# Two blocks with 32 experts on one core: fixed order of TensorE's side work, another place for the lasting slot, and loaded norm weights

## The chip, the cores and the metric

One core of a Trainium2 chip. The metric is the time of one execution on the device in microseconds (us). Engines are named as in the profile: PE is TensorE (matmuls; PEld its weight loads), DVE is VectorE, ACT is ScalarE, POOL is GpSimd, SP the engine whose queue issues the weight loads (SPq).

## The reference

256 tokens of width 1024 go through two transformer blocks in float32. The first is a hybrid layer (four mixers and a gated feed-forward part), the second has a pool and differential attention, cross attention and a mixture of experts, and a last RMS norm. The change touches only the mixture of experts and that norm:

```python
def clamped_swiglu(gu):
    gate, up = gu[..., :D_EXPERT], gu[..., D_EXPERT:]
    gate = jnp.minimum(gate, 7.0)
    up = jnp.clip(up, -7.0, 7.0)
    return (up + 1.0) * gate * jax.nn.sigmoid(1.702 * gate)

# 32 experts, each token goes to its top 4, gates = softmax over these four
hb = clamped_swiglu(xb @ w_gu[e] + b_gu[e])      # w_gu[e]: 1024 x 2048
yb = hb @ w_down[e] + b_down[e]                  # w_down[e]: 1024 x 1024
y = y.at[tok].add(yb * gate)
...
return rms_norm(x + y, final_norm_g)
```

All 32 experts' weights are read: 8 MB of gate/up and 4 MB of down weights each.

## The kernel before

The first three quarters of the text compute everything up to the router; the change leaves that alone but for one vector of norm weights (`load_vecs("v5", ...)`, line 577). The rest, from line 1320 on, is the expert stage.

**Tiles and products.** Each expert has 64 places for tokens (`CAP`). A gather (matmuls of the token rows `x_t` with a normalised one-hot matrix, lines 1459 and 1472) makes `xg`, the tokens of two experts at a time (`GR = 2`). The gate/up product "gu" (line 1524) runs over eight steps k; each step has four matmuls of 512 columns, and each shows as two instructions (eight per step, 64 per expert). ACT copies the result to `gs` (line 1532). `swiglu` turns it: `make(0)` and `make(1)` each transpose four blocks on PE (line 1541, tile "gte") and run seven operations on DVE and ACT (lines 1547 to 1555) into `u`. The down product "dn" (line 1567) has eight steps of two matmuls (32 instructions). `hilo` splits its result into `yh` (ACT, line 213) and `yl` (DVE, line 214), and `scatter` (line 1577) adds both to the four accumulators `acc` by a map `sT` that `turn_slots` makes on PE (lines 1444 to 1448, tile "ste").

**Order of an expert.** For expert e the text says: `make(0)`; the gate/up product of e + 1 with `make(1)` placed ahead of its step 1, the scatter of e - 1 ahead of step 3 and the slot map of e ahead of step 4; then the down product of e with, for even e, the two gathers for the next pair ahead of its steps 0 and 4. These places are the order of the text only. A planner in the framework chooses the real order of each engine by its own times and may move an instruction ahead of others. An *issue edge* (`with behind(m)`, which enters `tc.issue_after`) ties it: instructions of the block are put behind the given instruction on that instruction's engine; it adds no wait.

**Accumulators.** PSUM has eight banks here: four for `acc`, two of tag "mm", one "tr", one "y". gu uses both "mm"; dn uses "y"; transposes, slot maps and gathers use "tr", `make(1)` "y".

**Slots and loads.** Weights lie in a ring of 12 slots of 16 KB per partition (2 MB; `SLOTS`, `slot_tile`, line 1482), taken in turn. A gate/up set takes four, a down set two. SP's queue issues the loads (line 1494; the last piece of the last expert in three parts, line 1510), each when the readers of the slot's former content are done. Expert 30's `gs` must outlive the test below, and so is put into a slot of its own, "keep", taken just ahead of gu30; expert 30 and 31's remaining loads come behind it.

**The end.** After expert 29 stands `overflow()`: if any expert has more than 64 tokens, a loop works the rest off (line 1617 holds the test; here no body is run, but each engine branches past it). Behind it come 16 matmuls that spread the last norm's weights over the partitions (line 1679, tile "gb"), expert 30's `make`, gu31, dn30, dn31, the last scatters and the norm (lines 1696 to 1708).

Of the kernel before, what the change touches and what calls it, by code (L numbers as in the profile page):

```python
# [22 lines left out]
P = 128  # L23
T = 256
D = 1024
# [4 lines left out]
CAP = 64  # L30
# [13 lines left out]
def kernel(ctx: ExitStack, tc: tile.TileContext, A, out, probe=None, stop=None):  # L44
    nc = tc.nc
    V, S, G, PE = nc.vector, nc.scalar, nc.gpsimd, nc.tensor
    ld = nc.sync.dma_start
    ldc = nc.sync.dma_start
# [8 lines left out]
    last = {}  # L57
# [5 lines left out]
    @contextmanager  # L63
    def behind(m):

        with ExitStack() as es:
            for ins in m.values():
                es.enter_context(tc.issue_after(ins.ins))
            yield
# [21 lines left out]
    def ps(name, tag="mm"):  # L91
        return pst["pool"].tile([P, 512], F32, tag=tag, name=name, bufs=pst["tags"][tag])
# [38 lines left out]
    vec = {}  # L131
# [138 lines left out]
    def half(h):  # L270
        return slice(h * 512, (h + 1) * 512)
# [169 lines left out]
    for g0, g1 in ((0, 388), (388, 774), (774, 1160)):  # L441
        n = g1 - g0
# [58 lines left out]
    def attention(name, qk, kchunk, vcol, bias, sink=None, extra=None, cq=None):  # L501
# [3 lines left out]
        for p in range(4):  # L505
# [36 lines left out]
            for j in range(2):  # L542
                ptr = ps(f"{name}t{p}{j}", "tr")
                for b in (1, 0):
# [3 lines left out]
                    for s in range(b + 1):  # L548
# [28 lines left out]
    v5 = load_vecs("v5", [("attn", r128(A["attn_norm_g_2"]), 8), ("xattn", r128(A["xattn_norm_g_2"]), 8),  # L577
                     ("memn", r128(A["mem_norm_g_2"]), 8), *(("ffn", A["ffn_norm_g_2"].rearrange("o (k p j) -> (o k) p j", p=P, j=2)[:, :, j], 4) for j in range(2)),
                     ("pscale", r128(A["pool_scale_2"]), 4), ("subln", A["subln_g_2"], 1),
                     ("fgattn", A["final_g"].rearrange("(c p) -> c p", p=P), 8),  # L580
                     ("last", A["final_norm_g_2"].rearrange("(c p) -> c p", p=P), 8)])


    qc = qk_group("foxqk", 1792, 8, 4)
# [836 lines left out]
    def one_hot(pos_cols, n, name):  # L1421

        s_ = small.tile([P, 2, n, 2, CAP], BF16, tag="S_", name=f"S{name}", bufs=1)
        io = iota_s.unsqueeze(1).unsqueeze(1).to_broadcast([P, n, 2, CAP])
        for b in range(2):
            pos = pos_cols[:, b, :].unsqueeze(2).unsqueeze(3).to_broadcast([P, n, 2, CAP])
            V.tensor_tensor(s_[:, b], io, pos, op=ALU.is_equal)
        return s_
# [10 lines left out]
    def turn_slots(s_, g3, name):  # L1439

        pt = ps(f"st{name}", "tr")
        for b in range(2):
            sd = s_[:, b].rearrange("p q s -> p (q s)")
            PE.matmul(pt[:, b * P:(b + 1) * P], sd, ident_b, start=True, stop=True)  # L1444
            PE.matmul(pt[:, T + 3 * b:T + 3 * b + 3], sd, g3[:, b], start=True, stop=True)  # L1445
        S.copy(sT, pt[:, :T])
        gs_ = small.tile([P, 1], F32, tag="gslot", name=f"gslot{name}")
        V.tensor_reduce(out=gs_, in_=pt[:, T:T + 6], axis=AX.X, op=ALU.add)
        return gs_
# [32 lines left out]
    def slot_tile():  # L1482

        rawc[0] += 1
        pool = slots[SLOTS[slot[0] % len(SLOTS)]]
        slot[0] += 1
        return pool.tile([P, 4 * D], F32, tag="raw", name=f"raw{rawc[0]}")
# [13 lines left out]
    def load_gu(src, ahead=()):  # L1501
        w = [t.rearrange("p (j c) -> p j c", j=2) for t in ahead]
        return (w + [piece(src, m, slot_tile(), 2) for m in range(len(w), 4)]).__getitem__

    def load_dn(src, parts=False):
        w = [piece(src, m, slot_tile(), 4) for m in range(2 - parts)]
        if parts:
            t = slot_tile().rearrange("p (j c) -> p j c", j=4)
            for a, b in ((0, 2), (2, 3), (3, 4)):
                ld(t[:, a:b, :], src[4 * P:8 * P, :].rearrange("(p j) c -> p j c", j=4)[:, a:b, :])  # L1510
            w.append(t)
        return w.__getitem__

    def gu_product(wt, xg, col, name, between=None):

        pgu = [ps(f"gu{name}_{n}") for n in range(2)]
        for k in range(8):
            for f in (between or {}).get(k, ()):
                f()
            if k % 2 == 0:  # L1520
                w = wt(k // 2)
            for n in range(2):
                for cg in range(2):
                    PE.matmul(pgu[n][cg * CAP:(cg + 1) * CAP, :], xg[:, k, col:col + CAP],  # L1524
                              w[:, k % 2, cg * D + n * 512:cg * D + (n + 1) * 512], start=k == 0, stop=k == 7)
        return pgu

    def gu_out(pgu, name, gs=None):
        if gs is None:
            gs = small.tile([P, D], F32, tag="gs", name=f"gs{name}", bufs=1)  # L1530
        for n in range(2):
            S.copy(gs[:, n * 512:(n + 1) * 512], pgu[n])  # L1532
        return gs

    def swiglu(gs, bcol, name, u_=u_):

        def make(h, tag="tr"):
            pt = ps(f"gt{name}_{h}", tag)
            for c in range(4):

                PE.transpose(pt[:, c * P:(c + 1) * P], gs[:, every(4, 4 * h + c)], ident)  # L1541
            pv = pt.rearrange("p (c q s) -> p c q s", c=4, q=2)

            g_, t_ = (gs[:, 512 * h + 256 * i:512 * h + 256 * (i + 1)].rearrange("p (c s) -> p c s", c=4)
                      for i in range(2))
            u = u_[:, h]
            V.tensor_tensor(g_, pv[:, :, 0, :],  # L1547
                            bcol[:, 4 * h:4 * h + 4].unsqueeze(2).to_broadcast([P, 4, CAP]), op=ALU.add)
            V.tensor_tensor(u, pv[:, :, 1, :],
                            bcol[:, 8 + 4 * h:12 + 4 * h].unsqueeze(2).to_broadcast([P, 4, CAP]), op=ALU.add)  # L1550
            V.tensor_scalar(g_, g_, 7.0, None, op0=ALU.min)  # L1551
            V.tensor_scalar(u, u, 7.0, -7.0, op0=ALU.min, op1=ALU.max)
            S.activation(t_, g_, AF.Tanh, scale=0.851)  # L1553
            V.scalar_tensor_tensor(u, u, 1.0, g_, op0=ALU.add, op1=ALU.mult)
            V.scalar_tensor_tensor(u, t_, 1.0, u, op0=ALU.add, op1=ALU.mult)
        return make

    def dn_product(wt, gslot, name, u_=u_, tag="y", between=None):

        po = ps(f"dn{name}", tag)  # L1560
        for k in range(8):
            for f in (between or {}).get(k, ()):
                f()
            if k % 4 == 0:
                w = wt(k // 4)
            for cg in range(2):
                PE.matmul(po[cg * CAP:(cg + 1) * CAP, :], u_[:, k // 4, k % 4, :],  # L1567
                          w[:, k % 4, cg * 512:(cg + 1) * 512], start=k == 0, stop=k == 7)
        hilo(yh, yl, po, scale=gslot() if callable(gslot) else gslot)

# [19 lines left out]
        st["xg"], *how = gather(norm_hot(pos_cols, GR, f"g{g}"), GR, f"g{g}")  # L1590
        return how

    def front(e, between):
        if e == EOVER + 1:

            st["keep"] = slot_tile()
        w = load_gu(w_gu[e], () if e else gu0)
        pgu = gu_product(w, st["xg"], (e % GR) * CAP, f"e{e}", between)

        return gu_out(pgu, f"e{e}", st["keep"][:, :D] if e == EOVER + 1 else None)  # L1600

    def slots_of(e):
        st["gslot", e] = turn_slots(one_hot(pos1[:, :, e:e + 1], 1, f"e{e}")[:, :, 0], gate3[:, :, e, :], f"e{e}")

    chunk, _ = group(0)
    first = {k: [lambda k=k: chunk(k + 1, k % 2 == 0, ("tr", "y")[(k + 1) % 2])] for k in range(1, 7)}
# [38 lines left out]

    for e in range(NE - 2):
        make = swiglu(gs, bgu[:, :, e], f"e{e}")
        make(0)
        between = {1: [lambda: make(1, "y")], 4: [lambda: slots_of(e)]}
        if e and e - 1 != EOVER:  # L1650
            between[3] = [scatter]
        gs = front(e + 1, between)
        wd = load_dn(w_dn2[e])
        if e == 15:
            load_b_down()
        if e == EOVER:

            wg1 = load_gu(w_gu[e1])
            wd0, wd1 = load_dn(w_dn2[e0]), load_dn(w_dn2[e1], parts=True)
        if e == 2:  # L1660
            counts()
        between = {}
        if e % GR == 0:
            _, four = group(e // GR + 1)
            between = {0: [lambda: four(0)], 4: [lambda: four(1)]}
        if e == 15:
            between = {4: [gates_down], 6: [add_b_down]}
        dn_product(wd, st["gslot", e], f"e{e}", between=between)

    scatter()  # L1670
    overflow()


    work = slot_tile()
    gb2 = work[:, D:2 * D]
    for h in range(2):
        pt = ps(f"gb2_{h}")
        for c in range(4):
            PE.matmul(pt[:, c * P:(c + 1) * P], vec["last"][:, 4 * h + c:4 * h + c + 1].to_broadcast([P, P]), ident,  # L1679
                      start=True, stop=True)  # L1680
        S.copy(gb2[:, half(h)], pt)
    make = swiglu(gs, bgu[:, :, e0], f"e{e0}")
    make(0)
    slots_of(e0)
    gs = gu_out(gu_product(wg1, st["xg"], (e1 % GR) * CAP, f"e{e1}", {1: [lambda: make(1)]}), f"e{e1}")
    u1 = slot_tile()[:, :2 * 4 * CAP].rearrange("p (h c s) -> p h c s", h=2, c=4)
    make1 = swiglu(gs, bgu[:, :, e1], f"e{e1}", u1)
    dn_product(wd0, st["gslot", e0], f"e{e0}", between={2: [lambda: make1(0)], 4: [lambda: make1(1)]})
    dn_product(wd1, lambda: st["gslot", e1], f"e{e1}", u_=u1, tag="mm",
               between={2: [scatter], 4: [lambda: slots_of(e1)]})  # L1690
    ssl = mp.tile([P, 3, 2], F32, name="ssl")
# [49 lines left out]
```

## Time and profile before

| | us |
|---|---|
| median of 3 runs (lowest, highest) | 1718.88 (1717.53, 1719.52) |
| profiled execution | 1718.83 |
| its span, first to last instruction | 1717.1 |
| PE busy | 1613.4 (94%) |
| DVE busy | 721.5 (42%) |
| ACT busy | 510.9 (30%) |
| POOL busy | 221.1 (13%) |
| HBM read | 524.95 MB |

The span is that of the profiled execution; the time measured for the same execution is 1.7 us longer. Busy time of PE counts pipelined matmuls with modelled ends. In the rows below "idle before" and "<-" name what ended an engine's wait. The expert stage runs from about 760 us to the end.

### The profile page before, as it was taken

To read this page: it belongs to the slowest core of one execution; us is meant where nothing else is said; L and a number is where in the kernel's file an instruction comes from. 1 tells how busy PE (TensorE), PEld (TensorE's weight loads), DVE (VectorE), ACT (ScalarE), POOL (GpSimd) and SP (SyncE) were. 2 spreads that over 40 slices of the span, in tenths; PEclk is the share of its full clock that TensorE was granted. 3 is DMA by queue.
4 is the path that set the end of the run, shared out by engine and by line. 5 is a ranking of instruction groups with operands and counts; after the bars stand their busy time and mean duration, and the time that the engine had idled before them with its cause. 6 is when DMAs were issued, how large, how long until landed. Compare 5 with 4: busy or idle time off the path is not lost. (4 is left out here: it accounts for less than half of the span.)

```text
span 1717.1 us, 23092 instructions
## 1 busy us (share of the span) xinstructions
PE 1613.4 (94%) x9269; PEld 1013.2 (59%) x9270; DVE 721.5 (42%) x1613; ACT 510.9 (30%) x959; POOL 221.1 (13%) x319
## 2 busy tenths in 40 slices
PE   9899999999999999999999999999999999999987
PEld 8887799989999888974333333333333333333332
DVE  5867654667777775542222222212221212122113
ACT  4464554555555555521010111101100101110011
POOL 6988412200011000000000000000000000000000
PEclk9999999999999999999999999999999999999999
DMA  9842355655654535479999999999999999999972
GB/s 288 258 162 66 106 184 184 209 183 177 200 178 161 188 123 184 185 307 428 427 427 427 428 427 427 428 428 426 417 427 428 427 426 428 428 427 427 427 336 74
DMA packets 139316, 527.56 MB, mean 307 GB/s; under 512 B 11073, under 2 KB 99046, under 8 KB 114598
## 3 DMA queue, kind: packets, MB, share of 16 engines
q1 hardware_dynamic: 139206, 526.05, 77.8%
q8 instruction: 74, 1.21, 0.3%
q14 instruction: 36, 0.29, 0.1%
HBM read 524.95 MB, written 4.22 MB: 308 GB/s over the span
## 5 line engine op out<-in xcount | busy, mean ns | idle before, releaser
L1524 PE MATMUL gue<-raw,xgg 128*64 128x512 f32 x2032 | 452.8, 596 | 0.0
L189 DVE TENSOR_TENSOR wl<-raw,wh 128x1024 fp32r<-128x1024 f32 (+3 forms) x218 | 273.5, 1256 | 179.2 <-ACT wh L188 178.6
L188 ACT CAST wh<-raw 128x1024 fp32r<-128x1024 f32 (+2 forms) x220 | 227.8, 1035 | 259.1 <-PE g L197 64.6
L1524 PEld LDWEIGHTS gue<-raw,xgg 128*64 128x64 f32 x2032 | 139.8, 137 | 267.0 <-issue 262.8
L1567 PE MATMUL dne<-raw,u__8494 128*64 128x512 f32 x992 | 227.5, 598 | 0.0
L1532 ACT COPY gse<-gue 128x512 f32<-128x512 f32 x62 | 36.3, 585 | 328.2 <-PE gue L1524 328.2
L1567 PEld LDWEIGHTS dne<-raw,u__8494 128*64 128x64 f32 x992 | 66.0, 136 | 112.9 <-issue 107.3
L1547 DVE TENSOR_TENSOR gse<-gte,bgu 128x256 f32<-128x256 f32 x62 | 26.3, 424 | 232.5 <-PE gte L1541 232.5
L1701 POOL TENSOR_TENSOR ssl<-ssl,nhalf 128x1 f32<-128x1 f32 x2 | 1.1, 556 | 953.3 <-DVE ssl L1700 953.3
L1475 DVE TENSOR_TENSOR xgg<-xgg_h,v_c 128x512 f32<-128x512 f32 x30 | 20.7, 691 | 222.4 <-PE gue L1524 177.4
L1553 ACT ACTIVATE gse<-gse 128x256 f32<-128x256 f32 x62 | 25.8, 416 | 211.2 <-DVE gse L1551 211.2
L1472 PE MATMUL xgg_h<-SXg,x_t 128*128 128x128 f32 x480 | 64.8, 288 | 19.4 <-DVE xgg L1475 11.1
L1472 PEld LDWEIGHTS xgg_h<-SXg,x_t 128*128 128x128 f32 x480 | 58.9, 196 | 38.9 <-DVE xgg L1475 23.4
L388 POOL TENSOR_TENSOR convo<-convo,prod 128x256 f32<-128x256 f32 x90 | 76.9, 854 | 7.4
L196 PE MATMUL g<-h_h,wh 128*128 128x256 f32 x256 | 73.1, 286 | 0.0
L197 PE MATMUL g<-h_l,wh 128*128 128x256 f32 x256 | 73.1, 285 | 0.0
L198 PE MATMUL g<-h_h,wl 128*128 128x256 f32 x256 | 72.9, 285 | 0.0
L214 DVE SCALAR_TENSOR_TENSOR yl<-dne,gslote,yh 128x512 fp32r<-128x512 f32 x32 | 24.0, 750 | 113.7 <-ACT yh L213 113.7
L213 ACT ACTIVATE yh<-dne,gslote 128x512 fp32r<-128x512 f32 x32 | 22.0, 687 | 164.7 <-PE dne L1567 164.7
L387 POOL TENSOR_SCALAR prod<-hconv,v_c 128x256 f32<-128x256 f32 x90 | 67.8, 753 | 8.6
L1541 PEld LDWEIGHTS gte<-ident,gse 128*128 128x128 f32 x248 | 34.7, 209 | 42.2 <-issue 15.6
L196 PE MATMUL ffg<-h_h,wh 128*128 128x256 f32 x176 | 50.4, 287 | 0.0
(807 smaller groups left out, 3071.8 us busy)
## 6 DMA issues: line engine op xcount, KB each, us to landing
raw<-in_w_gu_dram SPq DMA_DIRECT2D x127, 2048.0 KB
raw<-in_w_down_dram SPq DMA_DIRECT2D x63, 2048.0 KB
raw<-in_w_in_dram SPq DMA_DIRECT2D x32, 1024.0 KB
raw<-in_w_up_dram SPq DMA_DIRECT2D x22, 1024.0 KB
raw<-in_w_down_dram SPq DMA_DIRECT2D x12, 1024.0 KB
raw<-in_w_out_dram SPq DMA_DIRECT2D x8, 1024.0 KB
raw<-in_w_ckv_dram SPq DMA_DIRECT2D x8, 1024.0 KB
raw<-in_w_in_dram SPq DMA_DIRECT2D x13, 512.0 KB
```

What stands on the lines that cost most here:

```text
L188: S.copy(hi, src)
L189: last["lo"] = (eng or V).tensor_sub(lo, src, hi.bitcast(F32))
L196: PE.matmul(o, wh[:, k, :], ah[:, k, :], start=first and k == 0, stop=False)
L197: PE.matmul(o, wh[:, k, :], al[:, k, :], start=False, stop=False)
L198: PE.matmul(o, wl[:, k, :], ah[:, k, :], start=False, stop=last and k == nk - 1)
L387: G.tensor_scalar(prod[0][:, :T], hconv[:, c, k:k + T], w, 0.0, op0=ALU.mult, op1=ALU.add)
L388: G.tensor_add(convo[:, c, :], convo[:, c, :], prod[0][:, :T])
L1472: PE.matmul(po[:, i * w:(i + 1) * w], x_t[:, b, every(2, 4 * h + i)], s_[:, b].rearrange("p o s -> p (o s)"), start=b == 0, stop=b == 1)
L1524: PE.matmul(pgu[n][cg * CAP:(cg + 1) * CAP, :], xg[:, k, col:col + CAP], w[:, k % 2, cg * D + n * 512:cg * D + (n + 1) * 512], start=k == ...
L1532: S.copy(gs[:, n * 512:(n + 1) * 512], pgu[n])
L1541: PE.transpose(pt[:, c * P:(c + 1) * P], gs[:, every(4, 4 * h + c)], ident)
L1567: PE.matmul(po[cg * CAP:(cg + 1) * CAP, :], u_[:, k // 4, k % 4, :], w[:, k % 4, cg * 512:(cg + 1) * 512], start=k == 0, stop=k == 7)
```

## The change

The last norm's weights are no longer among the vectors of "v5"; they are loaded by one broadcast DMA (512 KB) into a slot, and the "gb" matmuls go. In `gu_product` and `dn_product` every block of side work gets an issue edge behind the last matmul ahead of it (the new `m`):

```diff
@@ -1514,14 +1513,16 @@
     def gu_product(wt, xg, col, name, between=None):
 
         pgu = [ps(f"gu{name}_{n}") for n in range(2)]
+        m = {}
         for k in range(8):
-            for f in (between or {}).get(k, ()):
-                f()
+            with behind(m):
+                for f in (between or {}).get(k, ()):
+                    f()
             if k % 2 == 0:
                 w = wt(k // 2)
             for n in range(2):
                 for cg in range(2):
-                    PE.matmul(pgu[n][cg * CAP:(cg + 1) * CAP, :], xg[:, k, col:col + CAP],
+                    m["P"] = PE.matmul(pgu[n][cg * CAP:(cg + 1) * CAP, :], xg[:, k, col:col + CAP],
                               w[:, k % 2, cg * D + n * 512:cg * D + (n + 1) * 512], start=k == 0, stop=k == 7)
         return pgu
 
@@ -1558,13 +1559,15 @@
     def dn_product(wt, gslot, name, u_=u_, tag="y", between=None):
 
         po = ps(f"dn{name}", tag)
+        m = {}
         for k in range(8):
-            for f in (between or {}).get(k, ()):
-                f()
+            with behind(m):
+                for f in (between or {}).get(k, ()):
+                    f()
             if k % 4 == 0:
                 w = wt(k // 4)
             for cg in range(2):
-                PE.matmul(po[cg * CAP:(cg + 1) * CAP, :], u_[:, k // 4, k % 4, :],
+                m["P"] = PE.matmul(po[cg * CAP:(cg + 1) * CAP, :], u_[:, k // 4, k % 4, :],
                           w[:, k % 4, cg * 512:(cg + 1) * 512], start=k == 0, stop=k == 7)
         hilo(yh, yl, po, scale=gslot() if callable(gslot) else gslot)
```

The places of the side work are new, and the slots of the last experts are taken in another order; `make` of expert 30 moves ahead of the overflow test, with its result in the second half of "keep":

```diff
@@ -1590,17 +1593,15 @@
         st["xg"], *how = gather(norm_hot(pos_cols, GR, f"g{g}"), GR, f"g{g}")
         return how
 
-    def front(e, between):
-        if e == EOVER + 1:
-
-            st["keep"] = slot_tile()
-        w = load_gu(w_gu[e], () if e else gu0)
-        pgu = gu_product(w, st["xg"], (e % GR) * CAP, f"e{e}", between)
-
+    def front(e, between, w=None):
+        pgu = gu_product(w or load_gu(w_gu[e], () if e else gu0), st["xg"], (e % GR) * CAP, f"e{e}", between)
         return gu_out(pgu, f"e{e}", st["keep"][:, :D] if e == EOVER + 1 else None)
 
+    def hot(e):
+        st["hot"] = one_hot(pos1[:, :, e:e + 1], 1, f"e{e}")[:, :, 0]
+
     def slots_of(e):
-        st["gslot", e] = turn_slots(one_hot(pos1[:, :, e:e + 1], 1, f"e{e}")[:, :, 0], gate3[:, :, e, :], f"e{e}")
+        st["gslot", e] = turn_slots(st["hot"], gate3[:, :, e, :], f"e{e}")
 
     chunk, _ = group(0)
     first = {k: [lambda k=k: chunk(k + 1, k % 2 == 0, ("tr", "y")[(k + 1) % 2])] for k in range(1, 7)}
@@ -1645,47 +1646,51 @@
 
     for e in range(NE - 2):
         make = swiglu(gs, bgu[:, :, e], f"e{e}")
-        make(0)
-        between = {1: [lambda: make(1, "y")], 4: [lambda: slots_of(e)]}
-        if e and e - 1 != EOVER:
-            between[3] = [scatter]
-        gs = front(e + 1, between)
-        wd = load_dn(w_dn2[e])
+        hot(e)
+
+        between = {2: [lambda: make(0), lambda: make(1, "y")], 5: [lambda: slots_of(e)]}
+        if e:
+            between[5].insert(0, scatter)
+        if e == EOVER:
+
+            wg0, wd, wg1, wd0 = load_gu(w_gu[e0]), load_dn(w_dn2[e]), load_gu(w_gu[e1]), load_dn(w_dn2[e0])
+
+            st["keep"] = slot_tile()
+            gs = front(e + 1, between, wg0)
+        else:
+            gs = front(e + 1, between)
+            wd = load_dn(w_dn2[e])
         if e == 15:
             load_b_down()
-        if e == EOVER:
-
-            wg1 = load_gu(w_gu[e1])
-            wd0, wd1 = load_dn(w_dn2[e0]), load_dn(w_dn2[e1], parts=True)
         if e == 2:
             counts()
         between = {}
         if e % GR == 0:
             _, four = group(e // GR + 1)
-            between = {0: [lambda: four(0)], 4: [lambda: four(1)]}
+            between = {4: [lambda: four(0), lambda: four(1, "mm")]}
         if e == 15:
             between = {4: [gates_down], 6: [add_b_down]}
+        if e == EOVER:
+            wd1 = load_dn(w_dn2[e1], parts=True)
+            work = slot_tile()
+            gb2 = work[:, D:2 * D]
+            ldc(gb2, A["final_norm_g_2"].unsqueeze(0).broadcast_to([P, D]))
+
+            u0 = st["keep"][:, D + D // 2:2 * D].rearrange("p (h c s) -> p h c s", h=2, c=4)
+            make0 = swiglu(gs, bgu[:, :, e0], f"e{e0}", u0)
+            between = {4: [lambda: make0(0), lambda: make0(1, "mm")]}
         dn_product(wd, st["gslot", e], f"e{e}", between=between)
 
     scatter()
     overflow()
 
 
-    work = slot_tile()
-    gb2 = work[:, D:2 * D]
-    for h in range(2):
-        pt = ps(f"gb2_{h}")
-        for c in range(4):
-            PE.matmul(pt[:, c * P:(c + 1) * P], vec["last"][:, 4 * h + c:4 * h + c + 1].to_broadcast([P, P]), ident,
-                      start=True, stop=True)
-        S.copy(gb2[:, half(h)], pt)
-    make = swiglu(gs, bgu[:, :, e0], f"e{e0}")
-    make(0)
-    slots_of(e0)
-    gs = gu_out(gu_product(wg1, st["xg"], (e1 % GR) * CAP, f"e{e1}", {1: [lambda: make(1)]}), f"e{e1}")
-    u1 = slot_tile()[:, :2 * 4 * CAP].rearrange("p (h c s) -> p h c s", h=2, c=4)
+    hot(e0)
+    gs = gu_out(gu_product(wg1, st["xg"], (e1 % GR) * CAP, f"e{e1}", {4: [lambda: slots_of(e0)]}), f"e{e1}")
+    u1 = work[:, :2 * 4 * CAP].rearrange("p (h c s) -> p h c s", h=2, c=4)
     make1 = swiglu(gs, bgu[:, :, e1], f"e{e1}", u1)
-    dn_product(wd0, st["gslot", e0], f"e{e0}", between={2: [lambda: make1(0)], 4: [lambda: make1(1)]})
+    hot(e1)
+    dn_product(wd0, st["gslot", e0], f"e{e0}", u_=u0, between={4: [lambda: make1(0), lambda: make1(1, "mm")]})
     dn_product(wd1, lambda: st["gslot", e1], f"e{e1}", u_=u1, tag="mm",
                between={2: [scatter], 4: [lambda: slots_of(e1)]})
     ssl = mp.tile([P, 3, 2], F32, name="ssl")
```

## Rows read from the trace of the kernel before

**Rows 1.** Window of an ordinary pair of experts; its first line names the columns

```profile
core 0: us, PE busy (x) PEld busy (x) DVE busy (x) ACT busy (x) POOL busy (x), PEclk, DMA share, GB/s
1408.64:1467.05 58.41, 53.83 (x265) 21.26 (x265) 13.03 (x38) 6.12 (x12) 0.00 (x0) 1.00 1.01 428
```

**Rows 2.** The load queue's timeline; start us, us, engine, line, op, tiles, count

```profile
1408.64 11.21 SPq L1494 DMA_DIRECT2D raw<-in_w_gu_dram  x4
...
1467.05 11.21 SPq L1494 DMA_DIRECT2D raw<-in_w_gu_dram  x4
...
1678.80 0.34 SPq L1494 DMA_DIRECT2D raw<-in_w_down_dram  x1
```

**Rows 3.** TensorE's waits in two pairs, 1408.64 to 1525.46; us in total, times, longest

```profile
PE acc L1577 <- ACT yh L213: 3.2, 4, 0.8
PE ste L1444 <- DVE u__8494 L1549: 2.9, 4, 0.9
PE xgg_h L1472 <- DVE xgg L1475: 1.6, 2, 0.8
PE xgg_h L1472 <- DVE gslote L1448: 1.3, 2, 0.7
```

**Rows 4.** Windows of the end of the stage; columns as in Rows 1

```profile
1661.00:1664.00 3.00, 1.23 (x8) 0.36 (x6) 0.50 (x1) 0.00 (x0) 0.00 (x0) 1.00 0.68 284
1664.00:1667.00 3.00, 0.00 (x0) 0.00 (x0) 0.00 (x0) 0.00 (x0) 0.00 (x0) 0.71 0.56 218
1667.00:1670.00 3.00, 1.32 (x6) 1.35 (x7) 0.49 (x2) 0.00 (x0) 0.00 (x0) 0.50 0.19 74
1670.00:1679.00 9.00, 9.00 (x46) 4.94 (x46) 4.60 (x15) 2.37 (x5) 0.00 (x0) 0.88 0.00 0
...
1685.00:1688.00 3.00, 3.00 (x16) 1.01 (x14) 0.00 (x0) 0.01 (x1) 0.00 (x0) 1.00 0.17 71
```

**Rows 5.** TensorE's timeline at gu2, then at gu30, dn29 and the branch

```profile
817.58 3.65 PE L1524 MATMUL gue<-raw,xgg 128*64 128x512 f32 x16
...
1638.58 3.65 PE L1524 MATMUL gue<-raw,xgg 128*64 128x512 f32 x16
1642.16 0.50 PE L1577 MATMUL acc<-yl,sT 64*128 64x512 f32 x1
1642.59 10.52 PE L1524 MATMUL gue<-raw,xgg 128*64 128x512 f32 x48
1652.94 7.04 PE L1567 MATMUL dne<-raw,u__8494 128*64 128x512 f32 x32
...
1668.68 3.65 PE L1679 MATMUL gb<-ident,v_c 128*128 128x128 f32 x16 [6.39 <-PEq L1617]
```

**Rows 6.** The load queue's waits from 1600 us on; one of nine

```profile
SPq L1494 <- DVE u__8494 L1555: 8.2, 1, 8.2
```

**Rows 7.** The chain of waits that ended last; start us, us, what

```profile
1668.68 3.65 PE gb L1679 x16
1672.33 0.47 PE gte L1541 x4
...
1675.91 0.68 PE gte L1541 x4
...
1705.88 0.70 ACT yh L213
...
1706.60 0.76 DVE yl L214
```

**Rows 8.** Branches at line 1617, two engines; ns min/median/max, first and last start

```profile
L1617 POOLq COMPARE_BRANCH  x1: 45/45/45, 849.8 to 849.8; - x1
...
L1617 PEldq COMPARE_BRANCH  x1: 6062/6062/6062, 1662.2 to 1662.2; - x1
```

**Rows 9.** DMA queues from 1500 to 1600 us; packets, MB, share of 16 engines

```profile
q1 hardware_dynamic: 2930, 42.67, 100.4%
q8 instruction: 4, 0.07, 0.3%
```

More of the change, by code (lines that the diff above doesn't have):

```diff
@@ L579 @@
                      ("pscale", r128(A["pool_scale_2"]), 4), ("subln", A["subln_g_2"], 1),
-                     ("fgattn", A["final_g"].rearrange("(c p) -> c p", p=P), 8),
-                     ("last", A["final_norm_g_2"].rearrange("(c p) -> c p", p=P), 8)])
+                     ("fgattn", A["final_g"].rearrange("(c p) -> c p", p=P), 8)])
     qc = qk_group("foxqk", 1792, 8, 4)
```

## The prediction

> **What bounds the kernel now.** I read the stretches first. In an ordinary pair of experts the weight traffic runs at 428 GB/s with a DMA share of 1.01, and TensorE is busy 53.83 of 58.41 us [rows 1]: two resources look full at once, so the waits must tell which one leads. The queue that issues the loads starts the same four gate/up loads 58.41 us apart [rows 2]. One load is 2048 KB = 2.097 MB, 4.90 us at 428 GB/s; a pair has 12, 58.8 us. So the transfers are the slower by some 0.4 us per pair, yet all the idle time of TensorE in two pairs goes to ACT and DVE, none to a DMA [rows 3]: it runs far behind the data and waits for its own neighbours, 9.0 us in two pairs, 4.5 per pair.
>
> How far behind: the stream runs dry between 1661 and 1667, where 284 and 218 GB/s over 3 us each are 1.51 MB, 3.5 us at the full rate, so by the rate it would end at 1664.5 [rows 4]. Behind the last down weights of expert 29 it carries seven loads (four of gu31, one of dn30, two of dn31), 34.3 us: those landed at about 1630.2, and the first piece of gu30, five loads earlier, at 1605.7. TensorE starts gu30 at 1638.58 [rows 5]: 32.9 us late. The same count at gu2, 168 loads earlier, gives 782.5 against a start at 817.58 [rows 5]: 35.1 us. It carries this lag through the whole stage.
>
> At the end it becomes the tail. The stream is dry, one last load goes out only at 1678.80 [rows 2] (it waited 8.2 us for DVE, [rows 6]: the last reader of the "keep" slot) but is in by about 1685.5 [rows 4] and delays nobody; the chain is TensorE from 1668.68 to 1705.88, then 11.2 us of last scatter and norm [rows 7]. Before that stands a hole: TensorE's branch at the overflow test takes 6.062 us [rows 8].
>
> **The change part by part.**
>
> *Issue edges.* Transposes, slot maps and scatter of each expert now stand behind the second and fifth of eight steps of the gate/up product, gathers behind the fourth of the down product. Take the four waits of [rows 3]. "acc <- yh" (0.8 us per expert): the scatter came straight behind the down product; now 40 matmuls (8.6 us) stand between, against 0.70 + 0.76 us of evacuation [rows 7]. "xgg <- gslote" and "xgg <- xgg" (0.7 and 0.8 per pair): both gathers go to the down product's middle with a bank each ("tr", "mm"), so the second no longer waits for the first's evacuation. "ste <- u" (0.7): the slot map waited for the bank of the transposes; now 24 matmuls, 5.2 us, lie between. What is late next? The down product needs u; its DVE chain starts about 5 us into a product of 13.8, so it is covered. The next gate/up product needs the gathered rows: 16 matmuls (3.45 us) cover two DVE copies of 0.7 us. Added: runs that are broken. 16 matmuls before a break take 3.58 us (1638.58 to 1642.16), while 48 unbroken ones take 10.35, 3.45 per 16 [rows 5]; four more breaks per pair are 0.5 us. So a pair costs TensorE 53.8 + 0.5 = 54.3 us, if all 4.5 go. Bounds: nothing but the breaks to gain (54.3), or four new waits of the present size, 0.8 us each, in the four products: 57.5. I take 54.3, since each cover is several times its wait.
>
> Then TensorE gains 58.8 - 54.3 = 4.5 us per pair on the stream; 35.1 / 4.5 = 7.8 pairs, so it catches up near expert 18 and from there waits for weights. The pair remains 58.8: in the middle of the stage nothing is won, the lag is what goes.
>
> *Slots.* Before, "keep" was taken ahead of gu30 and the second piece of dn30 fell on its place in the ring of 12. Now keep is taken behind dn30, on gu30's first piece, and dn31 on gu30's second and third: every load is issued before the branch. The stream grows at its end by the 2 MB that used to come late: 1664.5 + 4.9 = 1669.4. The norm's weights are a 512 KB load on the slot of gu30's last piece, on SP's queue beside dn31's pieces: 0.5 / 2 of a load, 1.2 us, needed only in the last scatter; it costs nothing unless it gets ahead of dn31 (then 1.2 us on the stream, which has the slack shown below). The eight rows no longer loaded early are worth nothing here.
>
> *The end, in steps.* dn29's last piece lands at 1630.2. From packet to first matmul I estimate 1.0 us: the lone load issued at 1678.80 needed 4.9 us of transfer and ended about 1685.5, 1.8 us over, about half of it behind. Half a product, 3.65 us [rows 5]: 1634.8. From the end of dn29 to TensorE's return it was 1659.98 to 1668.68, 8.7 us (evacuation, scatter, branch): 1643.5. The tail was 1668.68 to 1717.1, 48.4 us. Gone are the 16 "gb" matmuls, 3.65, and expert 30's eight transposes, 0.47 + 0.68 [rows 7], which now fall into dn29's wait for its second piece: 43.6. But the granted clock is 0.50 after the branch, and the row 1670 to 1679 with 0.88 says that the lower level (1.2 GHz) lasts till about 1672.1 [rows 4]; those 3.4 us were spent on the norm's matmuls and will now fall on gu31's: 1.7 us more work left, 45.3. End 1643.5 + 45.3 = 1688.8. Weights allow it: dn30 starts near 1661 and its pieces land near 1655 and 1660, dn31's near 1665 and 1670 against starts near 1670 and 1675. The profiled execution took 1718.83 for a span of 1717.1, 1.7 more, and the median shown is 1718.88, the same within 0.1: **1690.5 us**.
>
> **Rivals.**
>
> *Weights set the end (faster still).* If the branch cost what it costs POOL (0.045 us, [rows 8]), TensorE would be back at 1637.5 and wait for weights to the end: 1669.4 + 1.0, the last step 0.9, then 11.2: 1682.5, time 1684. For it: the code's layout moves. Against: the jump crosses the same overflow body. 0.09.
>
> *The edges don't take the waits away.* The order is still made by a planner with its own times; a wait that moves is as good as one that stays. With 57.5 us per pair the lag at gu30 is 35.1 - 14 x 1.3 = 17 us; dn29 ends 21.4 us after gu30's start, at 1644, and the time is 1700. With nothing won only the tail's 48.4 - 45.3 = 3.1 us remain: 1715.7. Needed to catch up at all: 35.1 / 14 = 2.5 us per pair, that is 2.1 of the 4.5 (at 0.4 us already on its side, less the 0.5 of breaks). For it: several edges per expert must come out right. Against: each wait has its cover above. 0.13, of which 0.05 ends within 0.2% of no change.
>
> *The branch waits behind the weights (slower).* In the trace TensorE's branch began at 1662.2 [rows 8] and its next matmul ran at 1668.68, some 3 us after the stream ran dry; so its code may have waited for the queue to drain. Caught up, the branch begins near 1637 with eight or more loads queued. If the fetch waits for them all, it begins at 1669.4 + 1.2 and lasts 6.06 + 0.4: back at 1677.1, plus 45.3 and 1.7 is 1724: slower. It decides from a branch of about 33 us on (27 us over today's). Against it: with the weight queue at 100.4% for 100 us, instruction packets still came through, four in 100 us [rows 9]; a fetch that had to wait for an empty queue never would. 0.06.
> The Trainium skill (DMA: Bandwidth & Descriptors, Queues, rings and completion order) says that each DMA engine takes its queues in turn, packet by packet. By that the fetch loses a packet's time and the 1724 falls away; rows 9 agree, but no row shows a request's own delay.
>
> *The clock falls in the waits.* Caught up, TensorE waits up to 4.9 - 3.45 = 1.45 us per piece, where now it is idle 0.8 at a time with a granted clock of 1.00 [rows 1]. If a wait brings the 1.2 GHz level, 16 matmuls take 6.9 us, longer than a piece, so it stops waiting; it can lose one such stretch at the end, 1.7 us, and another in gu31: 1694. 0.04.
> The Trainium skill (TensorE: Matmul & The Clock Gate, HAM oscillation) speaks against this change here: matmuls in batches with DMA waits between them are what it shows falling to half clock at each wait. By it the 1694 is the likelier; the trace shows a fall behind the 6 us branch and none behind the 0.8 us waits, and nothing between.
>
> **How the numbers follow.** The forecast itself has 0.68, its own range 1686 to 1698 (landing estimate 0 to 2, branch 5 to 9, small waits in the tail). From what can be told from no change, 0.2% or 3.4 us, faster is under 1715.4: 0.68 + 0.09 + 0.04 + 0.08 = 0.89; same 0.05; slower 0.06. The range 1683 to 1706 leaves out the third rival, the poorer half of the second and a little of the forecast's edges: about 0.15 to 0.2.
>
> **What would show it.** Right: the waits of rows 3 gone and TensorE's idle time in the second half of the stage put down to the gate/up and down DMAs; issues of a pair still 58.8 us apart; gu30 starting near 1608 and dn29 ending near 1635; the weight traffic without a gap until about 1670, no load after the branch; TensorE back near 1643.5 and a tail of 45 us. Wrong: acc, ste or xgg still waiting for ACT and DVE by some 0.8 us and gu30 starting past 1620; a branch much longer than 6 us; a granted clock under 1.00 between experts 18 and 29.

## The result, and the profile after

The changed kernel takes 1695.09 us (median of 4 runs, 1693.68 to 1697.03) against 1718.2 us before: ratio 0.9865, 95% interval 0.9848 to 0.9883, 23 us gained. The profiled execution took 1694.64 us for a span of 1692.9 us.

All of TensorE's waits between 790 and 1640 us (waits view, columns as in [rows 3]), where before there were only its neighbours ACT and DVE:

```profile
PE dne L1570 <- DMA raw<-in_w_down_dram: 41.3, 32, 1.7
PE gue L1525 <- DMA raw<-in_w_gu_dram: 28.9, 27, 1.5
```

They are waits for weights, the first of them at 997 us, at expert 9. A pair of experts before that moment and one late in the stage (same columns as [rows 1]), and the four gate/up loads of the late one (as [rows 2]):

```profile
863.25:914.24 50.99, 50.99 (x266) 20.99 (x264) 12.40 (x38) 6.12 (x12) 0.00 (x0) 1.00 1.01 426
1423.57:1482.40 58.83, 52.37 (x264) 21.20 (x264) 12.41 (x38) 6.13 (x12) 0.00 (x0) 1.00 1.01 427
```

```profile
1423.57 15.03 SPq L1493 DMA_DIRECT2D raw<-in_w_gu_dram  x4
...
1482.40 15.04 SPq L1493 DMA_DIRECT2D raw<-in_w_gu_dram  x4
...
1635.96 10.12 SPq L1509 DMA_DIRECT2D raw<-in_w_down_dram  x3
1650.66 0.33 SPq L1677 DMA_DIRECT2D raw<-in_final_norm_g_dram  x1
```

As long as it trails, TensorE takes 50.99 us for a pair and waits for nothing. Later the loads of a pair are 58.83 us apart, as twelve transfers of 4.90 us need. SP passes its own branch at 1651.6, and no load comes behind it. The granted clock stays 1.00 with waits of 1.3 us per piece. TensorE around dn29 and the test, to be held against [rows 5]:

```profile
1611.18 3.60 PE L1525 MATMUL gue<-raw,xgg 128*64 128x512 f32 x16
...
1631.11 3.65 PE L1570 MATMUL dne<-raw,u__8493 128*64 128x512 f32 x16 [1.28 <-DMA raw<-in_w_down_dram]
1634.70 1.23 PE L1542 MATMUL gte<-ident,raw 128*128 128x128 f32 x8
1635.94 3.65 PE L1570 MATMUL dne<-raw,u__8493 128*64 128x512 f32 x16
...
1648.26 9.53 PE L1525 MATMUL gue<-raw,xgg 128*64 128x512 f32 x32 [6.35 <-PEq L1618]
```

gu30 starts at 1611.18 instead of 1638.58, and TensorE is back from the test at 1648.26 instead of 1668.68: 20.4 of the 24.2 us that the span lost. The branch is as long as before (compare [rows 8]):

```profile
L1618 PEldq COMPARE_BRANCH  x1: 6026/6026/6026, 1641.8 to 1641.8; - x1
```

The chain that ended last begins there (as [rows 7], without the "gb" and "gte" steps at its head):

```profile
1648.26 9.53 PE gue L1525 x32
...
1665.05 3.43 PE dne L1570 x16
1668.48 1.16 PE gte L1542 x8
1669.64 5.30 PE dne L1570 x24
...
1681.83 0.69 ACT yh L213
```

From 1648.26 to 1692.9 are 44.6 us against 48.4 before, the other 3.8. The end of the weight traffic, windows as in [rows 4]:

```profile
1667.00:1670.00 3.00, 3.00 (x18) 1.52 (x16) 0.73 (x3) 0.00 (x0) 0.00 (x0) 1.00 0.79 326
1670.00:1673.00 3.00, 3.00 (x16) 1.01 (x14) 2.86 (x11) 0.83 (x2) 0.00 (x0) 1.00 0.57 233
1673.00:1676.00 3.00, 3.00 (x18) 1.10 (x14) 0.90 (x2) 0.69 (x1) 0.00 (x0) 1.00 0.37 149
```

It doesn't stop, it fades, at a share of 0.79, 0.57 and 0.37, until 1676: some of the sixteen engines are done at 1668, others run on for 7 us more. Before it faded in the same way, from 1661 on [rows 4].

The kept trace also holds every DMA packet, and each engine ends its part of a load with one of 4 bytes. Followed from load to load, these sixteen ends of one load lie 2.0 us apart at 802 us, 3.5 at 1000, 4.8 at 1230, 6.6 at 1524 and 8.0 from 1611 on. For dn29's last piece the first engine ends at 1627.4, the last at 1635.4, and their average is 1630.9; TensorE goes on with it at 1635.94.

### The profile page after: what moved, and what is told of

It is laid out like the page before. It is cut to its first block, busy times and chain, and to the rows that moved or that the text cites. A ratio compares the mean times of both kernels' runs of the same rounds, so it can differ in the third digit from the quotient of the medians.

```text
span 1692.9 us, 23088 instructions
## 1 busy us (share of the span) xinstructions
PE 1582.4 (93%) x9253; PEld 1006.0 (59%) x9254; DVE 712.6 (42%) x1613; ACT 509.9 (30%) x957; POOL 221.2 (13%) x319
## 5 line engine op out<-in xcount | busy, mean ns | idle before, releaser
L1525 PE MATMUL gue<-raw,xgg 128*64 128x512 f32 x2032 | 464.0, 600 | 36.4 <-DMA raw<-in_w_gu_dram 28.9
L1570 PE MATMUL dne<-raw,u__8493 128*64 128x512 f32 x960 | 218.2, 596 | 41.3 <-DMA raw<-in_w_down_dram 41.3
L1570 PEld LDWEIGHTS dne<-raw,u__8493 128*64 128x64 f32 x960 | 70.9, 136 | 174.4 <-issue 168.4
L1426 DVE TENSOR_TENSOR Se<-iota_s,pos 128x128 bf16<-128x128 f32 x64 | 15.9, 288 | 131.3 <-PE ste L1444 124.4
L1445 ACT CAST sT<-ste 128x256 fp32r<-128x256 f32 x32 | 11.9, 372 | 161.8 <-PE ste L1444 161.8
L1471 PE MATMUL xgg_h<-SXg,x_t 128*128 128x128 f32 x480 | 60.5, 285 | 0.0
```

The source lines that it names most:

```text
L1471: PE.matmul(po[:, i * w:(i + 1) * w], x_t[:, b, every(2, 4 * h + i)], s_[:, b].rearrange("p o s -> p (o s)"), start=b == 0, stop=b == 1)
L1525: m["P"] = PE.matmul(pgu[n][cg * CAP:(cg + 1) * CAP, :], xg[:, k, col:col + CAP], w[:, k % 2, cg * D + n * 512:cg * D + (n + 1) * 512], st ...
L1570: m["P"] = PE.matmul(po[cg * CAP:(cg + 1) * CAP, :], u_[:, k // 4, k % 4, :], w[:, k % 4, cg * 512:(cg + 1) * 512], start=k == 0, stop=k == 7)
```

## The experiments

The theory was *lag*: TensorE trailed the weights by some 33 us because it waited for its neighbours; the new order removes the waits, it catches up, and dn29 ends when its weights are there. The rival was *end*: the gain comes from the slots, the norm's load and the earlier transposes.

**One half each.** The edges and places alone (with the second bank, "mm", among them), on the old slots and the old end:

```diff
-        make(0)
-        between = {1: [lambda: make(1, "y")], 4: [lambda: slots_of(e)]}
+        between = {2: [lambda: make(0), lambda: make(1, "y")], 5: [lambda: slots_of(e)]}
...
+            with behind(m):
...
-            between = {0: [lambda: four(0)], 4: [lambda: four(1)]}
+            between = {4: [lambda: four(0), lambda: four(1, "mm")]}
```

> The kernel before with the issue edges and the new places of side work only; slots, the norm's matmuls and the order behind the overflow test stay as before. Theory 'lag' (the edges remove TensorE's waits for its neighbours, it catches up with the weights, and the end moves with that): TensorE's waits for ACT and DVE gone from the pairs, dn29 ends near 1640 us as in the changed kernel (1639.5), TensorE back near 1648, then the old tail of 48.4 us: about 1698 us. Rival 'end' (the gain comes from the slots, the norm's load and the earlier transposes): over 1714 us.

Measured (edges_only): 1705.01 us, ratio 0.9927 (0.9908 to 0.9946): *lag* holds, but 7 us are missing. The waits for weights are there as in the changed kernel, TensorE is back from the test at 1646.62, and then (timeline, and windows of the same stretch):

```profile
1646.62 3.59 PE L1686 MATMUL gb<-ident,v_c 128*128 128x128 f32 x16 [6.68 <-PEq L1624]
...
1677.10 5.39 PE L1571 MATMUL dne<-raw,u__8494 128*64 128x512 f32 x16 [5.50 <-DMA raw<-in_w_down_dram]
```

```profile
1674.00:1677.00 3.00, 0.00 (x0) 0.00 (x0) 0.00 (x0) 0.00 (x0) 0.00 (x0) 0.50 0.68 289
1677.00:1680.00 3.00, 2.90 (x8) 0.99 (x10) 0.00 (x0) 0.00 (x0) 0.00 (x0) 0.50 0.00 0
```

dn30's second piece, the load that goes out behind the test, is awaited for 5.50 us, and the clock falls to the lower level (0.50, 1.2 GHz) in that wait; the 16 matmuls behind it take 5.39 instead of 3.65 us. The load that delayed nobody in the kernel before delays as soon as the lag is gone. The other half, new slots and end with the old order, one bank and no edges (edit against the changed kernel):

```diff
-            with behind(m):
+            with behind({}):
...
-        between = {2: [lambda: make(0), lambda: make(1, "y")], 5: [lambda: slots_of(e)]}
+        if e < EOVER + 1:
+            make(0)
+        between = {1: [lambda: make(1, "y")], 4: [lambda: slots_of(e)]}
...
-            between = {4: [lambda: four(0), lambda: four(1, "mm")]}
+            between = {0: [lambda: four(0)], 4: [lambda: four(1)]}
```

> The kernel before with the other half of the change: slots in the new order, the norm's weights loaded, expert 30's transposes ahead of the overflow test; no edges, old places of side work. Theory 'lag': gu30 still starts near 1638 us; the tail behind the test is 44.6 instead of 48.4 us: 1714 to 1716 us. Rival 'end': under 1700 us.

Measured (tail_only): 1715.27 us, ratio 0.9983 (0.9973 to 0.9992). Alone the halves are worth 12 and 3 us, together 23: the new slots are worth most where TensorE has no lag.

**Are the edges needed?** The changed kernel with its places but `behind({})`:

> The changed kernel with its new places in the text but without the issue edges. Theory 'lag' with the edges needed: the planner moves the work ahead again, waits of 0.7 to 0.9 us return at TensorE, 2 us or more per pair, and the time lies between 1703 and 1716 us. Rival 'places alone do it' (the second bank and the new places remove the waits whatever the edges do): within 3 us of the changed kernel's 1695.

Measured (no_edges): 1694.7 us (0.9865, 0.9849 to 0.9882): the rival is right as to the time, and my theory as to the waits, for they do return. All of TensorE's waits between 790 and 1720 us of more than 1 us in total:

```profile
PE acc L1580 <- ACT yh L213: 24.3, 31, 0.8
PE ste L1443 <- DVE u__8493 L1550: 15.7, 29, 1.0
PE xgg_h L1471 <- DVE gslote L1447: 7.9, 12, 0.7
PE gue L1525 <- PEq L1618: 6.6, 1, 6.6
```

No wait for weights, 24.3 + 15.7 + 7.9 us for neighbours; but "xgg <- xgg" of [rows 3] is missing. Its place in the text, or its second bank? I went on from tail_only, with the gather edit alone, then its two parts.

```diff
-            between = {0: [lambda: four(0)], 4: [lambda: four(1)]}
+            between = {4: [lambda: four(0), lambda: four(1, "mm")]}      # gather_only
+            between = {0: [lambda: four(0)], 4: [lambda: four(1, "mm")]} # bank_only
+            between = {4: [lambda: four(0), lambda: four(1)]}            # place_only
```

> The kernel tail_only (old places, no edges, new slots and end; 1715.3 us) plus one edit: both gathers ahead of step 4 of the down product, the second into a 'mm' bank. Theory 'the second bank does most of what the edges were thought to do': the pair falls from 58.4 to about 57 us, as in the kernel without edges (56.9), and the time to 1695 to 1701. Rival 'it is the places of transposes, slot map and scatter': the pair stays above 58 us and the time above 1710.

> tail_only (1715.3 us) plus the second bank alone: the second gather writes a 'mm' bank, both gathers stay at their old places in the text. Theory 'the bank is what counts' (the second gather waited 0.8 us for the first's evacuation, and so did what stood behind it): pair 56.9 us, time 1693 to 1697. Rival 'the place counts': pair 58.4, time 1713 to 1716.

> tail_only (1715.3 us) plus the new place alone: both gathers ahead of step 4 of the down product, both in the one bank 'tr'. Theory 'the bank is what counts': the wait of the second gather for DVE stays, pair 58.4, time 1713 to 1716. Rival 'the place counts': 1693 to 1697.

| kernel | us | ratio (95%) |
|---|---|---|
| tail_only | 1715.27 | 0.9983 (0.9973 to 0.9992) |
| place_only | 1715.12 | 0.9978 (0.9969 to 0.9988) |
| gather_only | 1694.45 | 0.9866 (0.9845 to 0.9888) |
| bank_only | 1695.97 | 0.9872 (0.9855 to 0.9888) |
| changed kernel | 1695.09 | 0.9865 (0.9848 to 0.9883) |

The bank does it all. One pair of gather_only, from gu to gu (TensorE's timeline), and its gu30 and dn29:

```profile
1414.55 3.65 PE L1525 MATMUL gue<-raw,xgg 128*64 128x512 f32 x16
...
1431.83 2.15 PE L1471 MATMUL xgg_h<-SXg,x_t 128*128 128x128 f32 x16
...
1471.47 3.65 PE L1525 MATMUL gue<-raw,xgg 128*64 128x512 f32 x16
...
1616.10 3.65 PE L1525 MATMUL gue<-raw,xgg 128*64 128x512 f32 x16
...
1632.00 7.09 PE L1570 MATMUL dne<-raw,u__8493 128*64 128x512 f32 x32
```

1414.55 to 1471.47 are 56.92 us against 58.41; the second gather follows its product without the 0.8 us wait. About 0.3 us more per pair come from shorter waits of the slot map ("ste": 20.3 us in all in tail_only, 15.7 here); where the rest comes from is not shown. 1.49 us in each of 14 pairs are 20.9 us, and tail_only less gather_only is 20.8.

It is a narrow thing, though. TensorE never waits for weights in gather_only, so it still trails: gu30 starts at 1616.10, 4.9 us behind the changed kernel's 1611.18. Then it runs gu30 and dn29 without a wait, where the changed kernel waits for their weights, and dn29 ends at 1639.1 against 1639.6. At this point the kernel before was 20.4 us late (its dn29 ended at 1659.98), and the bank saves 20.9: that these agree is luck of this kernel's size. And with the whole gather edit (second bank and place) on the kernel before:

> The kernel before plus only the gather edit (second bank and place); old slots, old end. Theory 'the gather edit closes the lag, and the old end then shows its late load': TensorE is back from the test near 1648 us, then the old tail of 48.4 plus up to 7 us of waiting for the load that goes out behind the test (5.5 us in edges_only): 1700 to 1706. Rival 'the old end costs only its 3.8 us of extra work': 1698.

Measured (gather_old_end): 1705.31 us (0.992, 0.9904 to 0.9937), with one wait of 3.51 us for the late load, as with the edges. The other way round, the changed kernel with `four(1)` back in "tr":

> The changed kernel with the second gather back in the one bank 'tr', edges and places kept. Theory 'edges and bank are two ways to the same end': one 0.8 us wait per pair comes back, the pair stays below the 58.8 us of the weights, TensorE still waits for weights in the second half, time 1694 to 1697. Rival 'the bank is needed in either case': TensorE keeps a lag and the time is over 1705.

Measured (edges_one_bank): 1695.68 us (0.9871, 0.9855 to 0.9887): the 0.8 us wait is back 15 times, 11.7 us, and TensorE waits that much less for weights. A pair before it catches up, columns as in [rows 1]:

```profile
864.93:916.98 52.05, 51.27 (x266) 21.08 (x264) 12.39 (x38) 6.13 (x12) 0.00 (x0) 1.00 1.01 426
```

So the edges and places alone bring TensorE's own pair from 58.4 to 52.05 us, the bank alone to 56.9, both together to 51.0. The edges close the lag, the bank all but closes it, and for the time either is enough.

**What would the edges be worth?** Half of each weight piece is loaded and used twice:

```diff
-        in_turn(t, src[n * m * P:n * (m + 1) * P, :].rearrange("(p j) c -> p (j c)", j=n))
+        c = src.shape[1]
+        in_turn(t[:, :n * c // 2], src[n * m * P:n * (m + 1) * P, :].rearrange("(p j) c -> p (j c)", j=n)[:, :n * c // 2])
...
-                              w[:, k % 2, cg * D + n * 512:cg * D + (n + 1) * 512], start=k == 0, stop=k == 7)
+                              w[:, 0, cg * D + n * 512:cg * D + (n + 1) * 512], start=k == 0, stop=k == 7)
...
-                          w[:, k % 4, cg * 512:(cg + 1) * 512], start=k == 0, stop=k == 7)
+                          w[:, k % 4 // 2, cg * 512:(cg + 1) * 512], start=k == 0, stop=k == 7)
```

> The changed kernel with half of each expert weight piece loaded and used twice (half of the sums' weights are left out), same instructions on TensorE, half the bytes. Theory 'weights bound the second half of the stage': TensorE waits for no DMA, a pair of experts takes 54.3 us (53.8 busy and 0.5 for the breaks) instead of 58.8, dn29 ends some 40 us earlier than in the changed kernel, time 1650 to 1662 us. Rival 'TensorE sets the pace also now': pairs stay near 58.8 us and the time near 1695.

Measured (half_after): 1606.28 us (0.9348, 0.9323 to 0.9374), further than expected. Its pair, as [rows 1]:

```profile
1323.02:1374.04 51.02, 51.02 (x267) 21.00 (x265) 12.41 (x38) 6.13 (x12) 0.00 (x0) 1.00 0.74 248
```

51.02 us, without a gap: that is TensorE's own pace in the new order, the same that the changed kernel shows with whole weights before it catches up (50.99), and 5.9 us under gather_only's. The expectation missed because it took 54.3. With whole weights the pair is held at 58.8 once TensorE has caught up, and all of this is spent waiting.

**What sets the end now?** Three kernels took the overflow test out of the way: with a loop around its three inner blocks (a shorter body to jump over), without it, and with it behind expert 19.

```diff
-                    for blk in range(1, T // CAP):      # test_small
+                    with tc.For_i(1, T // CAP, 1):
+                        blk = 1
...
-    overflow()                                          # no_test
...
+        if e == OV:                                     # test_early, OV = 19
+            scatter()
+            overflow()
```

> The changed kernel with the three blocks inside the overflow loop written as a loop of its own, so that the code jumped over is a third as long. Theory 'the 6 us branch is the fetch of code behind a long body': TensorE's branch at the test falls well under 6 us, it returns near 1642 instead of 1648, and the landing of the last weights (traffic until about 1675.5 in the changed kernel) sets the end: 1689 to 1691 us. Rival 'any jump over the loop costs the fetch': the branch stays at 6 us, time 1695.

Measured (test_small): 1694.66 us (0.9865, 0.9846 to 0.9885): TensorE's branch took 6.127 us over the shorter body, no less; the rival is right.

> The changed kernel without the overflow test and its loop (the work for tokens beyond 64 per expert is left out). Theory 'the landing of the last weights is the next bound': TensorE waits for the down weights of experts 30 and 31, time 1689 to 1691 us, 5 us less than the changed kernel although 7 us of standing still are gone. Rival 'the byte count says when weights land' (my prediction's reckoning): end of traffic at 1669.4, 1684 us.

Measured (no_test): 1691.09 us (0.984, 0.9821 to 0.986): the 6.35 us that TensorE stood still at the branch are gone, and the span is 2.9 us shorter. From gu31 on TensorE waits for weights again:

```profile
1641.66 3.65 PE L1525 MATMUL gue<-raw,xgg 128*64 128x512 f32 x16
...
1660.71 3.65 PE L1570 MATMUL dne<-raw,raw 128*64 128x512 f32 x16 [1.34 <-DMA raw<-in_w_down_dram]
...
1670.51 1.94 PE L1570 MATMUL dne<-raw,raw 128*64 128x512 f32 x8 [1.35 <-DMA raw<-in_w_down_dram]
```

So the landing of the last weights comes next, 1691 and not 1684.

> The changed kernel with the overflow test (and its untaken loop) behind expert 19 instead of expert 29, six loads issued ahead of it, and expert 29's scatter put into gu31. Theory 'lag': TensorE waits for weights there anyway and makes the 7 us good within two pairs; at the end nothing stands between dn29 and gu31, so the landing of the last down weights sets the end. The weight traffic of the changed kernel ran until about 1675.5 us (its slower half of engines): 1675.5 + 0.9 for the last step + 11.2 for scatter and norm + 1.7 = about 1689 us. Rival 'the branch is hidden already' (the 6 us cost nothing where they stand): 1695. Rival 'SP stops at the test and the stream runs dry there': 1696 to 1702 us, with a gap in the weight traffic behind expert 19.

Measured (test_early): 1698.29 us (0.9879, 0.9863 to 0.9896), the third of the expectations. Loads of SP's queue, and windows:

```profile
1325.42 5.22 SPq L1493 DMA_DIRECT2D raw<-in_w_down_dram  x2
1371.76 2.01 SPq L1493 DMA_DIRECT2D raw<-in_w_gu_dram  x4
```

```profile
1360.00:1370.00 10.00, 10.00 (x52) 3.33 (x52) 4.09 (x15) 1.21 (x3) 0.00 (x0) 1.00 0.69 295
1370.00:1380.00 10.00, 10.00 (x62) 5.75 (x60) 2.24 (x6) 1.17 (x2) 0.00 (x0) 1.00 0.72 275
```

Behind the test SP issues nothing before 1371.76, when TensorE has long been back (1353.08); the last of the loads issued ahead of the test has ended at 1370.4 (packets of the trace), so the stream runs dry. In this kernel the traffic at the end does not fade (compare the windows of the changed kernel above):

```profile
1673.00:1676.00 3.00, 2.47 (x12) 0.57 (x8) 2.19 (x7) 0.90 (x2) 0.00 (x0) 1.00 0.97 407
1676.00:1679.00 3.00, 2.17 (x10) 0.87 (x12) 0.75 (x1) 0.20 (x1) 0.00 (x0) 1.00 0.99 399
1679.00:1682.00 3.00, 3.00 (x22) 1.13 (x20) 0.00 (x0) 0.00 (x0) 0.00 (x0) 1.00 0.45 179
```

It stays at 0.97 and 0.99 until 1679 and is over by 1683, 300 us after the stream had been dry, where the changed kernel's, unbroken for 900 us, fades over 8. By the packets, the sixteen engines' ends of one load are 2.2 us apart at 1396 us, behind the dry stretch, and 3.7 at 1648.

No kernel here beats the changed one by more than its interval and computes all of it. With no_test, which leaves the test out, some 4 us are to be had there (the intervals of the two ratios overlap, but its slowest run, 1691.77, lies under the changed kernel's fastest, 1693.68).

## Why the prediction came out as it did

1690.5 was forecast, 1695.1 measured, inside the range of 1683 to 1706; 28.4 us of gain forecast, 23.1 measured.

- *TensorE's waits go, it catches up, and the pair stays at the weights' 58.8 us*: right. All of the four waits went in the changed kernel; the pair of loads is 58.83.
- *A pair then costs TensorE 54.3 us*: 51.0. I took the busy time of [rows 1], 53.83 us, as work, but the same instructions are busy for 50.99 us where they run in the new order. Probably the modelled ends of pipelined matmuls hide small drains in the longer figure; that is argued, not shown. Hence it caught up at expert 9, not 18. For the time it made no difference, as the weights set the pair.
- *The edges do it*: this was too much credit. I priced the four waits together, under the edges, though one of them goes by the second PSUM bank. That bank, one word, carries the whole gain without edges; without the bank the edges and places carry it too (edges_one_bank, 1695.68). The 5.9 us per pair by which both together are quicker than the bank alone fall into waits for weights. My own break-even (2.1 of 4.5 us needed) nearly said so; with the bank alone 1.5 us sufficed.
- *dn29's last piece lands at 1630.2, dn29 ends at 1634.8*: the term that was mis-sized. It ended at 1639.6 (1635.94 + 3.65), 4.8 us later, and this is more than the whole miss of the span (1692.9 against 1688.8). I counted bytes at the mean rate back from the end of the traffic. That count is good for the engines' average, 1630.9; but the piece is usable when the last of the sixteen has brought its part, at 1635.4, 4.5 us behind the average. [rows 4] showed the fading (0.68, 0.56, 0.19) that I read as an end at 1664.5; its third window (74 GB/s, 0.5 us at the full rate) I left out. The step from landing to matmul took 0.5 us where I had put 1.0. The same error made the lag too large by some 5 us, which is why 1.5 us per pair came so near to enough: 14 x (58.8 - 56.9) = 27 us, and 35.1 less 5 is 30.
- *From dn29's end to TensorE's return 8.7 us*: 8.7 (1639.6 to 1648.26). *Tail 45.3*: 44.6, the half-rate stretch of gu31 included.
- *The late load delays nobody*: true of the kernel before; caught up, it costs 3.5 to 5.5 us of waiting and a stretch at the lower clock.
- Rivals. *Weights set the end* was placed at 1684 by the same wrong count; without the test it is 1691. *The edges don't take the waits away* was true of no_edges for three of the four, where the time fell all the same.
- *The branch waits behind the weights*: not behind all of them, 6.026 us with a full queue ahead of it. But it may wait behind some: in half_after, where the weights had ended (DMA share 0.03 in the branch), it took 3.79 us, and the 16 KB instruction packet within it began 1.0 us after the branch did, against 3.5 us in the changed kernel (packets of the trace). One kernel without traffic is little to go by.
- *The clock falls in the waits*: no, 1.00 with 1.3 us waits. It was at 0.50 behind longer ones: 5.50 us in edges_only, 3.51 us in gather_old_end (16 matmuls 5.07 us), and the 6 us at the test. The Trainium skill (TensorE: Matmul & The Clock Gate, HAM oscillation) shows its falls in a kernel with longer waits for DMA than the 1.45 us to which I applied it; here it is borne out by the long waits only.

## What to carry to other kernels

Where a slower stream and an engine behind it both look full, count how far the engine trails: a saving of 1.5 us per pair was worth 21 us because the lag was about as large, and the next 5.9 us per pair were worth nothing. Before an ordering device gets the credit, give the buffers alone a run: a second bank for the second of two gathers did here what issue edges and new places were thought to do. A load that is late but unnoticed behind a lag must be moved together with the removal of the lag.

## What the runs showed of the hardware

- The engines of one DMA queue drift apart in a long unbroken stream. By the packets of the changed kernel the sixteen ends of one load were 2.0 us apart at 802 us and 8.0 at 1611, and the last loads faded out over 8 us. In test_early the spread was 2.2 us behind the dry stretch and 3.7 some 250 us later. It grows in steps, mostly of some 1.55 us on one engine at a time; what causes them is open. A load is complete with its slowest engine, for dn29's last piece 4.5 us behind the average.
- TensorE's branch past the overflow loop took 5.9 to 6.5 us in the twelve kernels in which weights were still coming, whether the body was long or a third as long, and 3.8 us in the one where they had ended (half_after, share 0.03); those of the other engines took 0.05 to 0.07 us.
- In test_early SP, past its branch since 1331, issued no load before 1371.76, when the loads issued ahead of the test had landed; the test in the midst of the stream cost a dry stretch.
